# A hybrid decoder step: a shared third PSUM bank and partition prices in the order model, output norms on VectorE, sample-state updates in one array visit

## The chip, the core and the metric

The kernel runs on one core of a Trainium2 chip. The time is the device time of one execution in microseconds (us), as the median of several runs; smaller is better. The engines are TensorE (PE, with its weight loads as PEld), VectorE (DVE), ScalarE (ACT), GpSimd (POOL) and SyncE (SP), whose queue issues the DMA transfers here.

## The reference, cut to what matters

One layer of a decoder is computed in float32 for two sets of tokens at once: a prompt of 16 meta tokens and 512 new ones, and 8 short sequences of 8 tokens that start from given states (the samples). 592 token columns go through one input projection `z = x @ w_in` (2048 to 8320). The first 4224 columns feed 16 heads of 64 of a recurrent mixer (RWKV-7), the other 4096 feed 8 heads of 128 of a retention mixer. Each head's output is normalised, gated, and goes into the output projection `w_out` (2048 x 2048), and a layer norm closes the layer:

```python
def step(S, inp):                       # RWKV-7, per token
    r_t, w_t, k_t, v_t, kk_t, b_t = inp
    sa = jnp.einsum('bhvk,bhk->bhv', S, -kk_t)
    S = S * w_t[:, :, None, :] + sa[..., None] * b_t[:, :, None, :] + v_t[..., None] * k_t[:, :, None, :]
    return S, jnp.einsum('bhvk,bhk->bhv', S, r_t)
...
h = jnp.einsum('btc,cd->btd', jnp.concatenate([o_a, o_b], axis=-1).astype(x.dtype), w_out)
y = _layer_norm(ALPHA * x + h, ln_g, ln_b)
```

Results are the outputs y of the prompt and of the samples, and all new states.

## The kernel before, in words

**Work and tiles.** The transposed tokens x are held in two parts whose sum is x (XH rounded, XL the rest), and each weight chunk is split in the same way into wh (ScalarE) and wl (VectorE). A projection is thus three wide matmuls per 128 rows of K: XH with wh, XL with wh, XH with wl. The input projection runs over 65 units of 128 output columns: one shared unit, then for each of 8 pairs of RWKV heads p the units k, r, v, g of that pair and q, k, v, g of retention head p. A unit has two halves of tokens (272 and 320), which go to the banks pj[0] and pj[1] (printed bank_115 and bank_116 below), 48 wide matmuls each.

**Jobs.** All other work of a pair is done by generators that run beside the projection of later units. `gen_a` prepares the keys and decays and makes the products inside chunks of 64 tokens: for each of the groups of chunks 0 to 3, 4 to 7, 8 to 9 it takes two banks and alternates matmuls on the upper and the lower 64 rows of the array (heads 0 and 1). `gen_u` inverts the triangular parts, `gen_c` runs the recurrence over 9 chunks, with three products in each that hand over to ScalarE or VectorE (copies RHS, ZZ, the new state), `gen_s` updates the states of the samples, `gen_f` normalises the heads. `gen_b` is the retention head; it updates the samples' retention states with two matmuls of 96 rows and 512 columns.

In `gen_s`, ScalarE copies a first product into RSv, TensorE transposes RSv, and after two more products VectorE makes ZX[h], the update vectors of the 8 samples side by side (8 x 64 columns) for head h. One matmul per head of 64 x 512 outputs goes to one half of the bank n0: head 0 into partitions 0 to 63, head 1 into 64 to 127.

**What sets the order.** Nothing is scheduled on the chip: each engine runs its instructions as they were written, in order, and they wait for each other by semaphores. The class `Order` decides the written order while the program is built. It keeps a modelled clock per engine and a table of who reads and writes what, and an operation's earliest time is the end of what it depends on, plus a lag (`LAG`) and, when TensorE is the reader, SLACK = 200 ns more. After each wide matmul `pump` lets every live job, by priority, emit what is ready by that clock; a batch of small matmuls that uses the array in another shape (fewer rows or columns than 128) is let in only when all of the batch is ready. `ensure` forces a job on when the projection needs its result. Small products share two banks, m0 and m1 (bank_117 and bank_118), through `take` and `give`; r0 and r1 are the retention's, ob (bank_120) the recurrence's outputs, and sq (bank_119) serves only the transposition of x at the start and the output projection.

**Output projection.** 16 K-chunks times 4 column blocks of 512 times 5 token tiles (four of 128 tokens, and tile 4 with the 64 sample tokens, whose extra product uses 64 columns of the array). In the last column block the matmuls of the last ten K-chunks are done tile by tile: tile 0 goes along, then tiles 1, 2, 3 and 4 are caught up one after the other. When a bank is done, VectorE adds alpha times x (`gen_cell`), takes statistics, and after the last block `gen_stat` makes the mean and, with two POOL operations, the reciprocal root of the variance. `gen_norm` then normalises the four blocks of the tile: by the table SHARE tiles 0 to 2 and half of tile 3 take one ScalarE step, a VectorE product with the gain and a POOL addition of the bias, the rest of tile 3 and tile 4 two fused VectorE steps. Each block is stored by SP.

In the profile of before, VectorE, ScalarE and POOL instructions carry the helper's line 363, matmuls the lines 386 and 392; in the changed kernel these are 380, 403 and 409.

Of the kernel before, what the change touches and what calls it, by code (L numbers as in the profile page):

```python
# [12 lines left out]
ACTF = mybir.ActivationFunctionType  # L13
ALU = mybir.AluOpType
# [14 lines left out]
NPAIR = 8  # L29
RAW_BUFS = 3  # L30
HI_BUFS = 4
SLACK = 200.0
AHEAD = -300.0
RUN = 1200.0
DRAIN = 90.0
LAND = 2400.0
LAND_BIG = 2400.0
LD = 4
# [1 line left out]
NPRIO = 1  # L40
OPRIO = 1
FIRST = 200.0
SHARE = "ggggggggggggggdddddd"
LATE = 5
EARLY = 14
BACKLOG = {0: 4000.0, 1: 1000.0, 2: 500.0, 3: 300.0, 4: 100.0}

_CSPEC = [("ident", 128), ("ind", 2), ("mS", 64), ("mSs", 64), ("mQ", 64), ("mQs", 64),
# [62 lines left out]
class Op:  # L111


    __slots__ = ("eng", "ns", "reads", "writes", "emit", "size")

    def __init__(self, eng, ns, reads, writes, emit, size=None):
        self.eng, self.ns, self.emit, self.size = eng, ns, emit, size
        self.reads, self.writes = [_box(a) for a in reads], [_box(a) for a in writes]


def _box(ap):


    t = ap.tensor
    dims = ap.ap
    if ap.space == bass.MemoryType.DRAM:
        return (t.name, 0, 1, ap.offset, ap.offset + sum((n - 1) * abs(s) for s, n in dims) + 1)
    if ap.space == bass.MemoryType.PSUM:
        return (t.name, -1, 0, 0, 1)
    pitch = 1  # L130
    for d in t.shape[1:]:
        pitch *= d
    p0, c0 = divmod(ap.offset, pitch)
    return (t.name, p0, p0 + dims[0][1], c0, c0 + sum((n - 1) * abs(s) for s, n in dims[1:]) + 1)


def _is_ap(x):
# [19 lines left out]
class Order:  # L157
# [6 lines left out]
    def __init__(self):  # L164
        self.clock = {k: 0.0 for k in ("PE", "DVE", "ACT", "POOL", "SP", "AQ", "DMA")}
        self.mem = {}
        self.job = None
        self.live = []
        self.stage = {}
        self.first = 0.0  # L170
        self.shape = (128, 128)
        self.tiles = [[0.0, 0.0] for _ in range(16)]
        self.issued = (0.0, 0.0)

    def lag(self, src, dst, raw):
        if src == dst:
# [3 lines left out]
    def ready(self, op):  # L180
# [7 lines left out]
                        t = max(t, end + self.lag(eng, op.eng, w and not isw))  # L188
        return t

    def emit(self, op):
        ns = op.ns
        start = max(self.clock[op.eng], self.ready(op))
        end = start + ns
        if op.eng == "PE":
            end = self.array(op, self.ready(op))
        self.clock[op.eng] = end
        if op.eng in ("SP", "AQ"):
            end = max(end + 1300.0, self.clock["DMA"]) + op.size / 270.0
# [207 lines left out]
def kernel(ctx, tc, x_prompt, x_sample, state_rwkv, state_shift, state_ret, meta_tokens, w_in, w_out,  # L407
# [138 lines left out]
    bank = [psum.tile([128, 512], F32, name=f"bank{i}") for i in range(8)]  # L546
    pj = [bank[0], bank[1]]
    m0, m1, sq, ob, r0, r1 = bank[2:]
    free = [m0, m1]

    o_d = dram.tile([16, 128, 576], F32, name="o_d")
    lt_d = [dram.tile([4, 10, 32, 32], F32, name=f"lt_d{i}") for i in range(2)]
# [23 lines left out]

    def give(*b):
        od.call(lambda: free.extend(b))

    lock = [1]  # L580

# [282 lines left out]
    def gen_s(p):  # L864
# [30 lines left out]
            tt(OO_[rows, 512:576], n0[rows, rows], RSs[64:128, rows], ALU.add)  # L895
        for h in range(2):
            tt(ZX[h], ZZ[:, 9, h, :].unsqueeze(1).to_broadcast([128, 8, 64]), C["bm"].unsqueeze(2).to_broadcast([128, 8, 64]))
            mm(n0[64 * h:64 * h + 64, :], BT[:, 9, h, :], ZX[h].rearrange("p b v -> p (b v)"))
        tt(S0T, n0, S0T, ALU.add)
        give(n0)  # L900
        mark(f"S{p}", 3)
# [189 lines left out]
    korder = [i for p in range(NPAIR) for i in ((p, 8 + p) if p < NPAIR - 1 else (8 + p, p))]  # L1091
    KO = len(korder)
    tiles = range(5)
    cells = [(n, t) for n in range(4) for t in tiles]
    j_in = len(chunks)
    for i in range(EARLY):
        events.append(("out", len(chunks), 0, i, (0, 1)))
        chunks.append(("out", korder[i], 0))
    for n in range(4):
        for i in range(KO):  # L1100
            events.append(("out", len(chunks), n, i, (2, 3, 4) if n == 0 and i < EARLY else tiles))
# [51 lines left out]
    with tc.manual_schedule():  # L1153
# [130 lines left out]
        def gen_stat(t):  # L1284
            rows = trows(t)
            mv = MV[0:rows, t, :]
            V.bn_aggr(out=mv, in_=ST6[0:rows, t].rearrange("p a b -> p (a b)"))
            rs = RSTD[0:rows, t:t + 1]
            ts(rs, mv[:, 1:2], 1.0, 1e-5, e=G)
            tt(rs, rs, NEGH[0:rows, 0:1], ALU.pow, e=G)  # L1290
            nm = NM[0:rows, t:t + 1]
            if set(SHARE[4 * t:4 * t + 4]) != {"d"}:
                stt(nm, mv[:, 0:1], -1.0, rs)
            od.call(lambda: od.start(f"N{t}", gen_norm(t), NPRIO))
            yield

        def gen_norm(t):
            rows = trows(t)
            rs, nm, mu = RSTD[0:rows, t:t + 1], NM[0:rows, t:t + 1], MV[0:rows, t, 0:1]
            dst = y_prompt[0, 128 * t:128 * t + 128, :] if t < 4 else xsamp_y  # L1300
            for n, step in ((0, 0), (1, 0), (0, 1), (2, 0), (1, 1), (0, 2), (3, 0), (2, 1), (1, 2), (3, 1), (2, 2), (3, 2)):
                sl = slice(512 * n, 512 * n + 512)
                hw = hh[0:rows, t, sl]
                who = SHARE[4 * t + n]
                if who == "d":
                    if step == 0:
                        stt(hw, hw, mu, lng[0:rows, sl], ALU.subtract, ALU.mult)
                    elif step == 2:
                        stt(hw, hw, rs, lnb[0:rows, sl], ALU.mult, ALU.add)
                elif step == 0:  # L1310
                    act(hw, hw, ACTF.Identity, rs, nm)
                elif step == 1:
                    tt(hw, hw, lng[0:rows, sl])
                else:
                    tt(hw, hw, lnb[0:rows, sl], ALU.add, e=G if who == "g" else V)
                if step == 2:
                    S.dma_start(out=dst[:, sl], in_=hw)
            yield

        xsamp_y = y_sample.rearrange("b t d -> (b t) d")  # L1320
# [25 lines left out]
        for e, ev in enumerate(events):  # L1346
            stage["event"] = e
            j = ev[1]
            if ev[0] == "in":
                _, j, u, half, q, ui = ev  # L1350
                kind, p, s = u
                if half == 0 and q == 0:
                    if kind == "A" and s == "k":
                        od.start(f"A{p}", gen_a(p), 1)
                    if kind == "B" and s == "q":
                        od.start(f"B{p}", gen_b(p), 3)
                if q == 0 and ui:
# [15 lines left out]
                        od.pump()  # L1373
            else:
                _, j, n, ki, some = ev
                od.ensure("o", ki + 1)
                if ki == 0:
                    if n == 0 and 4 in some:
# [7 lines left out]
                if n == 3 and ki >= KO - HELD:  # L1386
                    late += work[1:]
                    work = work[:1]
                    if ki == KO - 1:
                        work += sorted(late, key=lambda w: w[0])  # L1390
                for iw, (t, k_, jb) in enumerate(work):
                    b = obank[5 * n + t]
# [9 lines left out]
                    for i, (b_, x_, w_) in enumerate(todo):  # L1402
                        end = i == len(todo) - 1
                        mm(b_, x_, w_, start=(k_ == 0 and i == 0), stop=(k_ == KO - 1 and end))
                        if k_ == KO - 1 and end:
                            stage["out"] = 5 * n + t + 1
# [44 lines left out]
```

## Time and profile before

| | us |
|---|---|
| median of 3 runs (lowest, highest) | 1382.36 (1382.06, 1383.02) |
| the profiled execution | 1382.55 |
| its span, first to last instruction | 1380.8 |
| TensorE busy | 1331.4 |
| VectorE busy | 884.0 |
| ScalarE busy | 644.7 |
| POOL busy | 72.5 |

The mean granted TensorE clock is 0.991 of full speed. All times below are us from the start of the span. A row of the timeline gives the start, the length, engine, line, operation, `out<-in` by tile names, the part of the array (rows*columns) for matmuls, partitions x elements, how many equal instructions in a row it stands for, and in brackets the idle time ahead of it with the instruction that ended it. A float32 matmul that is not split appears as two records, one for each pass. A row of the stretches has the start and end, the length, then the busy time of PE, PEld, DVE, ACT and POOL, the granted clock, the DMA share and GB/s.

### The profile page before, as it was taken

How to read it: one execution, taken by the hardware profiler on the slowest of the kernel's cores; microseconds unless marked ns; L12 is line 12 of the kernel's file. 1: busy time of each engine (PE TensorE's matmuls, PEld its weight loads, DVE VectorE, ACT ScalarE, POOL GpSimd, SP SyncE). 2: the span in 40 equal slices, each digit the busy share in tenths (PEclk: the TensorE clock that was granted, in tenths of full speed). 3: DMA queues.
4: the chain of work that ended last, by engine and by line, in shares of the span. 5: the costliest groups of instructions: out<-in, count | busy, mean ns of one | idle time of the engine just before them, and what ended most of it. 6: DMA issues, size and time to landing. Idle time of an engine off the chain costs nothing.

```text
span 1380.8 us, 26964 instructions
## 1 busy us (share of the span) xinstructions
PE 1331.4 (96%) x10392; PEld 1230.1 (89%) x10392; DVE 884.0 (64%) x2158; ACT 644.7 (47%) x1519; POOL 72.5 (5%) x131
## 2 busy tenths in 40 slices
PE   7999999999999999999999999999999999999993
PEld 6999899989998999899989998999899987777782
DVE  5774677566766676667666765676567658624347
ACT  4534564366336633663356435643564366512121
POOL 0000000000000000000000000100010001000024
PEclk9999999999999999999999999999999999999997
DMA  7343224322432243224322432243224347654313
GB/s 238 87 109 90 69 74 118 94 66 72 118 87 73 66 123 85 75 65 120 84 81 64 118 80 81 63 118 85 80 62 120 88 138 214 195 166 117 98 48 122
DMA packets 232342, 139.79 MB, mean 101 GB/s; under 512 B 58668, under 2 KB 212102, under 8 KB 231238
## 3 DMA queue, kind: packets, MB, share of 16 engines
q1 hardware_dynamic: 232214, 138.08, 35.3%
q8 instruction: 81, 1.33, 0.4%
q14 instruction: 47, 0.39, 0.1%
HBM read 119.30 MB, written 18.74 MB: 100 GB/s over the span
## 4 chain that ended last, share of the span: by engine, by line
PE 81%; DVE 9%; ACT 6%; issue 3%; DMA 0%; POOL 0%; DVEq 0%; SPq 0%; ACTq 0%; POOLq 0%
PE bank L386 77%; DVE RW L363 5%; PE bank L392 4%; DVE wl L363 1%; ACT RW L363 1%; ACT SF L363 1%; ACT XH L363 1%; DVE MOM L363 1%; ACT RT L363 1%; ACT RHS L363 1%; ACT wh L363 1%; DVE RT L363 1%; ACT RSv L363 1%; DVE SHT L363 1%; DVE XL L363 0%
## 5 line engine op out<-in xcount | busy, mean ns | idle before, releaser
L386 PE MATMUL bank<-XH,wl 128*128 128x320 f32 (+3 forms) x2080 | 634.0, 305 | 2.1 <-DVE wl L363 2.1
L386 PE MATMUL bank<-XL,wh 128*128 128x320 f32 (+3 forms) x2080 | 629.1, 302 | 0.0
L386 PE MATMUL bank<-XH,wh 128*128 128x320 f32 (+3 forms) x2080 | 627.5, 302 | 1.2 <-ACT wh L363 1.2
L386 PEld LDWEIGHTS bank<-XL,wh 128*128 128x128 f32 x2080 | 391.9, 188 | 7.9 <-issue 6.3
L386 PEld LDWEIGHTS bank<-XH,wl 128*128 128x128 f32 x2080 | 392.9, 189 | 6.0 <-DVE wl L363 3.6
L386 PEld LDWEIGHTS bank<-XH,wh 128*128 128x128 f32 x2080 | 392.8, 189 | 3.0 <-ACT wh L363 1.4
L363 DVE TENSOR_TENSOR wl<-raw,wh 128x512 fp32r<-128x512 f32 x292 | 201.4, 691 | 203.0 <-ACT wh L363 200.1
L363 ACT ACTIVATE wh<-raw 128x512 fp32r<-128x512 f32 x292 | 184.1, 631 | 205.3 <-PE bank L386 178.6
L363 DVE TENSOR_TENSOR RW<-RW 120x84 f32<-120x84 f32 (+27 forms) x558 | 149.9, 272 | 19.5 <-ACT RW L363 4.0
L386 PE MATMUL bank<-RW 32*32 32x32 f32 (+6 forms) x1904 | 146.8, 242 | 2.9 <-DVE RW L363 2.0
L386 PEld LDWEIGHTS bank<-RW 32*32 32x32 f32 (+4 forms) x1904 | 108.9, 145 | 28.0 <-DVE RW L363 9.0
L363 ACT ACTIVATE RW<-bank 128x512 f32<-128x512 f32 (+8 forms) x218 | 93.2, 438 | 47.2 <-PE bank L392 33.3
L363 ACT ACTIVATE RT<-bank 64x320 f32<-64x320 f32 (+9 forms) x122 | 47.7, 398 | 126.4 <-DVE RT L363 102.7
L363 ACT ACTIVATE SF<-RW,FT 64x64 f32<-64x64 f32 x144 | 49.7, 345 | 71.1 <-DVE RW L363 69.2
L386 PE MATMUL bank<-more,XH 128*128 128x512 f32 (+1 forms) x250 | 75.9, 395 | 0.0
L363 ACT ACTIVATE RW<-bank,OMM 128x272 f32<-128x272 f32 (+1 forms) x66 | 33.2, 502 | 68.9 <-PE bank L386 67.4
L386 PE MATMUL bank<-wh,XH 128*128 128x512 f32 x157 | 62.0, 396 | 0.0
L392 PE MATMUL bank<-CT,RW 128*128 128x128 f32 (+2 forms) x348 | 53.7, 282 | 8.2 <-DMA RW<-in_x_prompt_dram 7.5
L386 PE MATMUL bank<-wl,XH 128*128 128x512 f32 (+1 forms) x157 | 61.6, 394 | 0.0
L386 PEld LDWEIGHTS bank<-more,XH 128*128 128x128 f32 (+1 forms) x250 | 45.6, 183 | 12.4
L363 DVE TENSOR_TENSOR RW<-bank,N 64x128 f32<-64x128 f32 x80 | 22.5, 282 | 46.8 <-PE bank L386 45.7
L392 PEld LDWEIGHTS bank<-CT,RW 128*128 128x128 f32 (+2 forms) x348 | 41.2, 139 | 10.4 <-issue 7.5
(154 smaller groups left out, 1397.3 us busy)
## 6 DMA issues: line engine op xcount, KB each, us to landing
raw<-in_w_in_dram SPq DMA_DIRECT2D x259, 256.0 KB
raw<-in_w_out_dram SPq DMA_DIRECT2D x48, 256.0 KB
CT<-in_w_out_dram SPq DMA_DIRECT2D x30, 256.0 KB
RT<-in_state_ret_dram SPq DMA_DIRECT2D x8, 512.0 KB
out_dram<-RT SPq DMA_DIRECT2D x8, 512.0 KB
RW<-in_x_prompt_dram SPq DMA_DIRECT2D x16, 256.0 KB
out_dram<-RW SPq DMA_DIRECT2D x16, 256.0 KB
RW<-o_d SPq DMA_DIRECT2D x14, 288.0 KB
```

Source lines behind the costliest of these rows:

```text
L363: self.order.submit(Op(self.key, self.cost(name, n, kw, psum), reads, [out], lambda: f(*args, **kw)))
L386: lambda: self.eng.matmul(out, lhsT, rhs, start=start, stop=stop), (passes, move, load, shape, tiles)))
L392: lambda: self.eng.transpose(out, in_, ident), (1, move, _cols(in_) / 1.2, shape, tiles)))
```

## The change

1. The order model: SLACK goes from 200 to 100 ns; a new price SWITCH of 110 ns stands ahead of a VectorE or ScalarE operation whose first partitions (of its output and its first input) differ from those of the operation before it on that engine.
2. Bank sq joins m0 and m1 as a third shared bank; a job takes it back (`gen_keep`) when unit g of the last RWKV pair starts, and the output projection waits for that.
3. In `gen_s` the two 512-column matmuls become eight of 128 columns that alternate between the heads, after both ZX are made.
4. The last column block is done in the tile order 4, 0, 1, 2, 3. Tile 4 goes along with the K-chunks, tiles 0 to 3 are caught up after it.
5. The norms take neither ScalarE nor POOL: for each tile VectorE does four steps with the mean and the gain, then four with the reciprocal root and the bias. The stores become jobs of their own.

```diff
-SLACK = 200.0
+SLACK = 100.0
+SWITCH = 110.0
-SHARE = "ggggggggggggggdddddd"
+TURN = (4, 0, 1, 2, 3)
+KEEP = ("A", 7, "g")
...
+        self.rows = tuple(_row(a) for a in writes + reads[:1])
...
+    def switch(self, op):
+        return SWITCH * (op.eng in ("DVE", "ACT") and self.rows.get(op.eng) != op.rows)
...
     def emit(self, op):
         ns = op.ns
-        start = max(self.clock[op.eng], self.ready(op))
+        start = max(self.clock[op.eng] + self.switch(op), self.ready(op))
+        self.rows[op.eng] = op.rows
...
-    free = [m0, m1]
+    free = [m0, m1, sq]
...
+    def gen_keep(b):
+        while not any(x is b for x in free):
+            yield
+        free[:] = [x for x in free if x is not b]
+        yield
...
         for h in range(2):
             tt(ZX[h], ZZ[:, 9, h, :].unsqueeze(1).to_broadcast([128, 8, 64]), C["bm"].unsqueeze(2).to_broadcast([128, 8, 64]))
-            mm(n0[64 * h:64 * h + 64, :], BT[:, 9, h, :], ZX[h].rearrange("p b v -> p (b v)"))
+        for i in range(4):
+            for h in range(2):
+                mm(n0[64 * h:64 * h + 64, 128 * i:128 * i + 128], BT[:, 9, h, :], ZX[h][:, 2 * i:2 * i + 2].rearrange("p b v -> p (b v)"))
...
-    cells = [(n, t) for n in range(4) for t in tiles]
+    cells = [(n, t) for n in range(4) for t in (TURN if n == 3 else tiles)]
...
-            for n, step in ((0, 0), (1, 0), (0, 1), (2, 0), (1, 1), (0, 2), (3, 0), (2, 1), (1, 2), (3, 1), (2, 2), (3, 2)):
-                ...
+            for n in range(4):
+                stt(hh[0:rows, t, cut(n)], hh[0:rows, t, cut(n)], mu, lng[0:rows, cut(n)], ALU.subtract, ALU.mult)
+            for n in range(4):
+                stt(hh[0:rows, t, cut(n)], hh[0:rows, t, cut(n)], rs, lnb[0:rows, cut(n)], ALU.mult, ALU.add)
+                od.call(lambda n=n: od.start(f"W{t}{n}", gen_put(dst[:, cut(n)], hh[0:rows, t, cut(n)]), 0))
...
+                    if (kind, p, s) == KEEP:
+                        od.start("keep", gen_keep(sq), 0)
...
-                        work += sorted(late, key=lambda w: w[0])
+                        work += sorted(late, key=lambda w: TURN.index(w[0]))
```

What this moves on the engines is shown at three places. The first is VectorE at the end of the program (RW holds the outputs, SHT the statistics). Before:

```order
L363 SCALAR_TENSOR_TENSOR RW<-RW,bank_121 64x512
L363 TENSOR_TENSOR RW<-bank_121,RW 64x512
L363 BN_STATS SHT<-RW 64x6
L363 BN_AGGR SHT<-SHT 64x2
L363 TENSOR_TENSOR RW<-RW 128x512 x2
L363 SCALAR_TENSOR_TENSOR RW<-RW,SHT 64x512 x4
L363 SCALAR_TENSOR_TENSOR RW<-RW,SHT 128x512
L363 SCALAR_TENSOR_TENSOR RW<-RW,SHT 64x512 x2
```

Now:

```order
L380 BN_AGGR SHT<-SHT 64x2
L380 SCALAR_TENSOR_TENSOR RW<-RW,SHT 64x512 x8
L380 SCALAR_TENSOR_TENSOR RW<-RW,bank_119 128x512
L380 BN_STATS SHT<-RW 128x6
L380 BN_AGGR SHT<-SHT 128x2
L380 SCALAR_TENSOR_TENSOR RW<-RW,SHT 128x512 x8
L380 SCALAR_TENSOR_TENSOR RW<-RW,bank_115 128x512
```

The 64-row tile stands before the four full ones, and each tile's eight norm steps follow its statistics in one piece, where steps of two tiles stood mixed before.

The second place is TensorE at the samples' state update of a middle pair (the rows with 64x512 before, 64x128 now). Before:

```order
L386 MATMUL bank_115<-XH,wl_106 128x272
L386 MATMUL bank_117<-RW 64x512
L386 MATMUL bank_118<-RW 128x128
L386 MATMUL bank_115<-XH,wh_102 128x272
L386 MATMUL bank_117<-RW 64x512
L386 MATMUL bank_115<-XL,wh_102 128x272
```

Now:

```order
L403 MATMUL bank_116<-XH,wl_106 128x320
L403 MATMUL bank_119<-RW 64x128 x8
L403 MATMUL bank_118<-RHS,RW 66x128
L403 MATMUL bank_116<-XH,wh_102 128x320
L403 MATMUL bank_116<-XL,wh_102 128x320
```

The two updates with a wide matmul between them became one piece of eight.

The third place is TensorE at the first group of chunk products of `gen_a` in the pair after it, eight matmuls that alternate between two banks. Now (before, the eight stood in one piece in every pair):

```order
L403 MATMUL bank_117<-RW 128x128
L403 MATMUL bank_118<-RW 128x128
L403 MATMUL bank_117<-RW 128x128
L403 MATMUL bank_118<-RW 128x128
L403 MATMUL bank_117<-RW 128x128
L403 MATMUL bank_115<-XH,wh_105 128x272
L403 MATMUL bank_118<-RW 128x128
L403 MATMUL bank_117<-RW 128x128
L403 MATMUL bank_118<-RW 128x128
L403 MATMUL bank_115<-XL,wh_105 128x272
```

A wide matmul now stands after the fifth of the eight; this is so in six of the eight pairs. The second group keeps its eight in one piece.

More of the change, by code (lines that the diff above doesn't have):

```diff
@@ L111 @@
 class Op:
-    __slots__ = ("eng", "ns", "reads", "writes", "emit", "size")
+    __slots__ = ("eng", "ns", "reads", "writes", "emit", "size", "rows")
     def __init__(self, eng, ns, reads, writes, emit, size=None):
         self.eng, self.ns, self.emit, self.size = eng, ns, emit, size
+        self.rows = tuple(_row(a) for a in writes + reads[:1])
         self.reads, self.writes = [_box(a) for a in reads], [_box(a) for a in writes]
@@ L134, in _box, with _row @@
     return (t.name, p0, p0 + dims[0][1], c0, c0 + sum((n - 1) * abs(s) for s, n in dims[1:]) + 1)
+def _row(ap):
+    pitch = 1
+    for d in ap.tensor.shape[1:]:
+        pitch *= d
+    return ap.offset // pitch
 def _is_ap(x):
@@ L173, in __init__ @@
         self.issued = (0.0, 0.0)
+        self.rows = {}
     def lag(self, src, dst, raw):
@@ L1093 @@
     tiles = range(5)
-    cells = [(n, t) for n in range(4) for t in tiles]
+    cells = [(n, t) for n in range(4) for t in (TURN if n == 3 else tiles)]
+    index = {c: i for i, c in enumerate(cells)}
     j_in = len(chunks)
@@ L1100 @@
         for i in range(KO):
-            events.append(("out", len(chunks), n, i, (2, 3, 4) if n == 0 and i < EARLY else tiles))
+            events.append(("out", len(chunks), n, i, (2, 3, 4) if n == 0 and i < EARLY else TURN if n == 3 else tiles))
             chunks.append(("out", korder[i], n))
@@ L1290, in gen_stat, with gen_put @@
             tt(rs, rs, NEGH[0:rows, 0:1], ALU.pow, e=G)
-            nm = NM[0:rows, t:t + 1]
-            if set(SHARE[4 * t:4 * t + 4]) != {"d"}:
-                stt(nm, mv[:, 0:1], -1.0, rs)
             od.call(lambda: od.start(f"N{t}", gen_norm(t), NPRIO))
+            yield
+        def gen_put(dst, src):
+            S.dma_start(out=dst, in_=src)
             yield
@@ L1298, in gen_norm @@
             rows = trows(t)
-            rs, nm, mu = RSTD[0:rows, t:t + 1], NM[0:rows, t:t + 1], MV[0:rows, t, 0:1]
+            rs, mu = RSTD[0:rows, t:t + 1], MV[0:rows, t, 0:1]
             dst = y_prompt[0, 128 * t:128 * t + 128, :] if t < 4 else xsamp_y
-            for n, step in ((0, 0), (1, 0), (0, 1), (2, 0), (1, 1), (0, 2), (3, 0), (2, 1), (1, 2), (3, 1), (2, 2), (3, 2)):
[L1302 to L1317, printed above, removed]
+            cut = lambda n: slice(512 * n, 512 * n + 512)
+            for n in range(4):
[3 more added lines that the diff above has]
+                od.call(lambda n=n: od.start(f"W{t}{n}", gen_put(dst[:, cut(n)], hh[0:rows, t, cut(n)]), 0))
             yield
@@ L1375 @@
                 _, j, n, ki, some = ev
+                od.ensure("keep", 99)
                 od.ensure("o", ki + 1)
@@ L1389 @@
                     if ki == KO - 1:
-                        work += sorted(late, key=lambda w: w[0])
+                        work += sorted(late, key=lambda w: TURN.index(w[0]))
                 for iw, (t, k_, jb) in enumerate(work):
-                    b = obank[5 * n + t]
+                    b = obank[index[n, t]]
                     if k_ == 0 and b in pj:
@@ L1405 @@
                         if k_ == KO - 1 and end:
-                            stage["out"] = 5 * n + t + 1
+                            stage["out"] = index[n, t] + 1
                         if iw == len(work) - 1 and end:
```

## The prediction

> **What bounds the kernel now.** I read the page's busy shares and chain first, then the table of stretches, then TensorE's own waits, then the last 50 us row by row.
>
> ```profile
> PE 1331.4 (96%) x10392; PEld 1230.1 (89%) x10392; DVE 884.0 (64%) x2158; ACT 644.7 (47%) x1519; POOL 72.5 (5%) x131
> PE 81%; DVE 9%; ACT 6%; issue 3%; DMA 0%; POOL 0%; DVEq 0%; SPq 0%; ACTq 0%; POOLq 0%
> 400.00:440.00 40.00, 38.68 (x376) 36.36 (x375) 18.60 (x45) 22.01 (x65) 0.21 (x1) 1.00 0.25 64
> 1357.20:1380.80 23.60, 0.00 (x0) 0.00 (x0) 18.40 (x21) 1.52 (x2) 8.90 (x9) 0.56 0.33 114
> ...
> PE bank L392 <- DMA RW<-in_x_prompt_dram: 7.5, 1, 7.5
> PE bank L386 <- ACT wh L363: 5.5, 7, 1.2
> PE bank L386 <- ACT RHS L363: 3.2, 10, 1.1
> PE bank L392 <- ACT RSv L363: 2.8, 8, 0.4
> PE bank L386 <- DVE wl L363: 2.1, 7, 0.6
> PE bank L386 <- DVE RW L363: 2.0, 8, 0.7
> ```
>
> TensorE is busy for 96% of the span. In a stretch from the middle it idles 1.3 of 40 us, at a granted clock of 1.00. So until TensorE's last matmul time is saved in two ways only: shorter occupation of the array, or removal of some of the waits in the last five rows (15.6 us together; the 7.5 us ahead of them is the first load). After 1357.20 TensorE does nothing, and 23.6 us follow in which VectorE is busy for 18.4. That tail is bound by VectorE and whatever it waits for.
>
> **The tail: norms on VectorE alone, small tile first.** The rows of VectorE at the first two token tiles of the last column block, TensorE's last matmul, and then tile 4 (64 rows) with what follows:
>
> ```profile
> 1331.72 0.69 DVE L363 SCALAR_TENSOR_TENSOR RW<-RW,bank 128x512 f32<-128x512 f32 x1 [5.83 <-PE bank L386]
> 1332.44 0.69 DVE L363 BATCH_NORM_STATS2 SHT<-RW 128x6 f32<-128x512 f32 x1
> 1333.17 0.26 DVE L363 BATCH_NORM_AGGREGATE SHT<-SHT 128x2 f32<-128x24 f32 x1
> ...
> 1338.68 0.69 DVE L363 SCALAR_TENSOR_TENSOR RW<-RW,bank 128x512 f32<-128x512 f32 x1 [0.16 <-PE bank L386]
> ...
> 1356.81 0.39 PE L386 MATMUL bank<-wh,XH 128*128 128x512 f32 x1
> ...
> 1361.52 0.67 DVE L363 SCALAR_TENSOR_TENSOR RW<-RW,bank 64x512 f32<-64x512 f32 x1
> 1363.67 0.26 DVE L363 BATCH_NORM_AGGREGATE SHT<-SHT 64x2 f32<-64x24 f32 x1
> 1365.65 6.58 DVE L363 SCALAR_TENSOR_TENSOR RW<-RW,SHT 64x512 f32<-64x512 f32 x2
> 1372.16 5.37 DVE L363 SCALAR_TENSOR_TENSOR RW<-RW,SHT 64x512 f32<-64x512 f32 x8
> ...
> 1364.01 1.10 POOL L363 TENSOR_SCALAR SHT<-SHT 64x1 f32<-64x1 f32 x1 [4.66 <-DVE SHT L363]
> 1365.20 0.94 POOL L363 TENSOR_TENSOR SHT<-SHT,NEGH 64x1 f32<-64x1 f32 x1
> 1366.11 4.91 POOL L363 TENSOR_TENSOR RW<-RW 128x512 f32<-128x512 f32 x4
> ```
>
> Two things are to be seen. The tile that TensorE finished at 1357.20 reaches VectorE only at 1361.52. And the row at 1365.65 holds two instructions in 6.58 us where eight of the same kind take 5.37 a little later: it stands beside POOL's four additions, 4.91 us, which the change removes.
>
> Worked out for the new order: a full tile costs VectorE 1333.43 - 1331.72 = 1.71 us to read the bank and make the statistics, and eight norm steps 5.37: 7.08. Tile 4 costs 1363.93 - 1361.52 + 5.37 = 7.78. From tile 4's last matmul on VectorE has 7.78 + 4 x 7.08 = 36.1 us to do. TensorE then has the four deferred tiles before it, each 1338.68 - 1331.72 = 6.96: 27.8. So VectorE ends 8.3 us after TensorE. All ScalarE steps of the norms are gone; ScalarE was not the limit there (1.52 us busy), and its work now costs VectorE nothing extra, as two fused steps replace three.
>
> To this comes POOL: two tiny operations per tile still make the reciprocal root. The first took 1.10 us beside VectorE's work and delayed nothing visible; the second ended at 1366.14, 0.49 us after the VectorE step of 1365.65 began. I take that row, 0.5 x 5 tiles = 2.5 us. The bounds are 0 (the four steps that need only the mean, 2.7 us, cover them) and both in full, 5 x 2.04 = 10.2. Behind VectorE's end stand 1380.80 - 1377.53 = 3.3 us of stores and closing, to which I add 0.5 since the last stores are now 256 KB and not 128. New tail 8.3 + 2.5 + 3.8 = 14.6 against 23.6: **9.0 us less** (12.0 less without interference and with 3.3; 1.3 less at the bad end).
>
> [...]
>
> **The state update: one visit.** Between the wide projection matmuls TensorE visits a job's small matmuls; what a visit costs is the time from the start of the wide matmul ahead of it to the next wide start, less one wide step (0.13, from 496.65 to 496.78 below).
>
> ```profile
> 444.07 0.37 PE L386 MATMUL bank<-XH,wh 128*128 128x272 f32 x1
> 444.37 1.07 PE L386 MATMUL bank<-RW 128*64 128x512 f32 x2
> 445.37 0.40 PE L386 MATMUL bank<-XL,wh 128*128 128x272 f32 x1
> ...
> 488.66 0.30 PE L386 MATMUL bank<-XH,wh 128*128 128x320 f32 x1
> 488.89 1.16 PE L386 MATMUL bank<-RW 64*128 64x128 f32 x16
> 489.98 0.41 PE L386 MATMUL bank<-XL,wh 128*128 128x320 f32 x1
> ...
> 496.65 0.29 PE L386 MATMUL bank<-XH,wh 128*128 128x258 f32 x1
> 496.78 0.28 PE L386 MATMUL bank<-XL,wh 128*128 128x258 f32 x1
> 496.99 0.89 PE L386 MATMUL bank<-RW 64*128 64x128 f32 x8
> 497.81 0.38 PE L386 MATMUL bank<-XH,wl 128*128 128x258 f32 x1
> ```
>
> One 512-column update (two passes, half the array's columns) costs 445.37 - 444.07 - 0.13 = 1.17 us, and there are two of them in each of eight pairs: 2.34 a pair. The new visit has eight updates of 128 columns, in turn on the two column halves. The trace has no such visit; the nearest is the one at 488.89: eight matmuls of 128 columns in two passes, in turn on the two row halves: 489.98 - 488.66 - 0.13 = 1.19. If the column halves run side by side like the row halves, a pair saves 1.15: **9.2 us less** in all. The bounds are 0 (no overlap: as much streaming as before) and 14 (a visit of 0.6, by the column-half visit in the next fence, which streams 32 columns).
>
> ```profile
> 429.97 0.55 PEld L386 LDWEIGHTS bank<-RW 128*64 128x64 f32 x16 [0.19 <-issue]
> ...
> 429.97 0.66 PE L386 MATMUL bank<-RW 128*64 128x32 f32 x16
> ```
>
> [...]
>
> **The new order of the rest.** The halved slack, the priced partition changes and the third bank move nearly every small job. Three consequences can be priced.
>
> First a cost: the order shown above splits the visit of eight row-half matmuls into five and three, in six of the eight pairs. Four such matmuls cost 497.81 - 496.78 - 0.13 = 0.90, eight 1.19: 0.07 for each and 0.61 for going in and out. Six more visits cost **3.7 us more**.
>
> Second a gain: two waits of before get more cover.
>
> ```profile
> L386 PE MATMUL bank<-XH 96*128 96x512 f32 x16 | 7.6, 473 | 4.7 <-ACT wh L363 4.3 <-ACT SF L363 0.4
> ...
> 480.07 0.56 ACT L363 ACTIVATE RW<-bank,VEC 64x256 f32<-64x256 f32 x1
> 480.66 0.53 ACT L363 ACTIVATE RW<-bank,OMM 128x320 f32<-128x320 f32 x1
> 481.09 0.43 ACT L363 ACTIVATE RW<-bank 128x320 f32<-128x320 f32 x1
> ```
>
> The retention state update (96 rows) waits 4.7 us in all and the transpose of RSv 2.8. By the two orders, 15 wide matmuls lie between the product that RSv is copied from and its transpose in a middle pair before, and 30 now. The partition price is real: ScalarE's instruction at 480.66 follows one on other partitions and starts 0.03 us after its end, the one at 481.09 stays on its partitions and starts 0.10 before the end, so the change costs 0.13; the model now charges 0.11 where it charged nothing, and that is what those waits were short of. Of the 7.5 us I take **4 less**; the bounds are 0 and 7.5.
>
> Third a cost: handoffs to TensorE are placed 0.1 us closer to their data. The recurrence alone has 9 chunks x 3 handoffs x 8 pairs = 216. Most pass through an instruction whose partition change is now charged, which gives the tenth back. I take **2 more**, with 0 and 216 x 0.1 = 21.6 as bounds. The third bank is costed at nothing: in the middle TensorE never stood still for a bank, it took other jobs' matmuls and the wide ones; if that cover failed, a wait would show on it as in the rows above.
>
> **Sum.** The profiled execution took 1382.55 us, of which the span is 1380.8; it is 0.19 above the median of the three runs. 1382.55 - 9.0 - 9.2 + 3.7 - 4 + 2 = 1366.05, against the median 1366.
>
> **Rivals.**
> POOL keeps blocking the norm steps: the tail at its bad end, 1.3 instead of 9.0 saved: 1374. For it the 6.58 us row, against it that this row had four large POOL operations behind the small ones. Chance 0.08.
> The column halves do not overlap: 9.2 us are missing, 1375. [...] Chance 0.06.
> The waits go nearly altogether: of the 15.6 us all but the 1.2 and 0.6 of the start vanish and no new ones come: 1382.55 - 9.0 - 9.2 + 3.7 - 13.8 = 1354. For it that the model now charges what it left out; against it the halved slack. Chance 0.08.
> Late handoffs, the slower side: in the recurrence each handoff comes 0.1 us too early and TensorE stands still for it, with the wide matmuls queued behind in its order: 1382.55 - 9.0 - 9.2 + 3.7 + 21.6 = 1390. It takes the whole gain from 14.5 / 216 = 0.067 us a handoff on. For it the 3.2 us that TensorE already waits for RHS; against it that this was ten waits out of all the handoffs. Chance 0.05.
> No difference: gains in the array are given back as waits elsewhere and the tail falls short. 0.03.
>
> **How the numbers follow.** The forecast itself, 0.70, has its own range of 1361 to 1371 (about 3 us either way for the tail and about 4 for the waits). To leave out no more than two in ten the range goes to 1357 on one side, half way to the vanished waits and beyond, and to 1375 on the other, where two rivals end. Differences under 0.2%, 2.8 us, count as none. Faster: 0.70 + 0.08 + 0.06 + 0.08 = 0.92; same 0.03; slower 0.05.
>
> **What would show it.** Tail: TensorE's last matmul some 14 to 15 us before the end, VectorE without a step above 1.3 us there, four tiles' norms 7 to 7.6 us apart. State: one visit per pair of 16 column-half passes of 128 columns, its matmuls in couples some hundredth of a microsecond apart, about 1.2 us long. Split: 30 row-half visits, not 24. Waits: those for RSv and for the 96-row update below half, the sum for RHS not above 5 us. Wrong it would be if RHS and DVE waits grew beyond 10 us, or VectorE's end lay more than 12 us behind TensorE's.

## The result and the profile after

The changed kernel takes 1345.17 us (median of 4, 1345.04 to 1347.60) against 1382.69 (4, 1382.06 to 1383.52) for the kernel before on the same chip: a ratio of 0.9732, 95% interval 0.9716 to 0.9749. The gain is 37.5 us; the forecast was 16.7, and its range ended at 1357. The profiled execution has a span of 1343.3 us at a mean clock of 0.997.

The page's busy times of the kernel after:

```profile
PE 1309.4 (97%) x10488; PEld 1230.2 (92%) x10488; DVE 879.8 (65%) x2168; ACT 634.4 (47%) x1505; POOL 55.3 (4%) x117
```

Its stretches, the one from the middle that the prediction showed of before, and the tail:

```profile
400.00:440.00 40.00, 40.00 (x401) 38.04 (x400) 23.83 (x62) 24.20 (x73) 1.58 (x3) 1.00 0.28 77
1329.30:1343.30 14.00, 0.01 (x1) 0.00 (x0) 8.20 (x13) 0.00 (x0) 1.68 (x2) 0.69 0.57 207
```

Its TensorE's own waits (us in total, times, longest):

```profile
PE bank L409 <- DMA RW<-in_x_prompt_dram: 7.6, 1, 7.6
PE bank L403 <- DVE RW L380: 4.7, 8, 1.1
PE bank L403 <- ACT RHS L380: 2.8, 3, 1.3
...
PE bank L409 <- ACT RSv L380: 0.3, 1, 0.3
```

The tail is 14.0 us (23.6 before). That leaves 37.5 - 9.6 = 27.9 us ahead of it: TensorE's last matmul ends at 1329.3 instead of 1357.2. The two waits that the prediction priced have gone (RSv 2.8 to 0.3; the 96-row update 4.7 to 0.1, a row further down), but the idle time in such lists is far too small to hold 27.9 us. Over the whole list it fell by some 5.

A second measure finds it, the one that the prediction used for single visits: from the start of the wide matmul ahead of a visit to the next wide start, less one wide step (0.147 us for 320 columns). It holds the visit's waits too. Summed over all visits of the input projection it is 245.7 us before (472 visits) and 213.8 after (460): 31.9 less. Between wide matmuls without a visit 5.0 us more are saved. Against that, the part from the input projection's last wide matmul to TensorE's last matmul became 8.5 us longer (219.8 to 228.3), and the start 0.5: 31.9 + 5.0 - 8.5 - 0.5 = 27.9. In that part the rest of the last pair's jobs runs beside the output projection; more of them is left now (137 small matmuls, 119 before), and all three waits for RHS of the list above lie there, between 1101 and 1161. The prediction has no term for it.

The 31.9 us are not seen in the idle column because a record is longer than a step, as TensorE's rows of the kernel before show:

```profile
432.78 0.31 PE L386 MATMUL bank<-XL,wh 128*128 128x320 f32 x1
432.92 0.31 PE L386 MATMUL bank<-XH,wl 128*128 128x320 f32 x1
433.95 0.47 PE L386 MATMUL bank<-XH 96*128 96x512 f32 x1 [0.72 <-ACT wh L363]
```

Wide matmuls start 0.14 us apart, so the 96-row one could have started at 433.07. It started at 433.95, 0.88 us late; the row owns up to 0.72, since a record of 0.31 us covers the first 0.16. Waits shorter than that don't appear at all, and TensorE counts as busy in them. A wait inside a visit can stay unseen in the same way. Eight row-half matmuls, the kind of which the prediction priced one visit at 1.19 us, stand in the same pair of the kernel before a second time:

```profile
492.27 0.31 PE L386 MATMUL bank<-XL,wh 128*128 128x320 f32 x1
492.51 1.41 PE L386 MATMUL bank<-RW 64*128 64x128 f32 x16
493.85 0.42 PE L386 MATMUL bank<-XH,wl 128*128 128x320 f32 x1
```

This visit costs 493.85 - 492.27 - 0.147 = 1.43 us: its second matmul, on the other row half, begins 0.25 us after the first, at 492.76, when a VectorE step has ended at 492.71; in the visit at 488.89 the two start 0.01 us apart. No idle time is booked. In the kernel after, all ten undivided visits of this kind cost about 1.18.

VectorE's rows at the end of the kernel after:

```profile
1309.32 0.69 DVE L380 SCALAR_TENSOR_TENSOR RW<-RW,bank 128x512 f32<-128x512 f32 x1
1316.38 0.68 DVE L380 SCALAR_TENSOR_TENSOR RW<-RW,bank 128x512 f32<-128x512 f32 x1
...
1330.48 0.68 DVE L380 SCALAR_TENSOR_TENSOR RW<-RW,bank 128x512 f32<-128x512 f32 x1
...
1332.22 5.39 DVE L380 SCALAR_TENSOR_TENSOR RW<-RW,SHT 128x512 f32<-128x512 f32 x8
```

Tiles follow 7.06 us apart, and VectorE ends at 1337.61, 8.3 us behind TensorE. TensorE's rows at the state update of a middle pair:

```profile
436.85 0.30 PE L403 MATMUL bank<-XH,wl 128*128 128x320 f32 x1
437.08 1.09 PE L403 MATMUL bank<-RW 128*64 128x128 f32 x16
438.11 0.43 PE L403 MATMUL bank<-RHS,RW 128*66 128x128 f32 x2
438.30 0.40 PE L403 MATMUL bank<-XH,wh 128*128 128x320 f32 x1
```

The new state visit, with a recurrence product in the same visit, costs 438.30 - 436.85 - 0.15 = 1.30 us.

### The profile page after: what moved, and what is told of

Its sections match the earlier page's. It is cut to its first block, busy times and chain, and to the rows that moved or that the text cites. A ratio compares the mean times of both kernels' runs of the same rounds, so it can differ in the third digit from the quotient of the medians.

```text
span 1343.3 us, 27153 instructions
## 1 busy us (share of the span) xinstructions
PE 1309.4 (97%) x10488; PEld 1230.2 (92%) x10488; DVE 879.8 (65%) x2168; ACT 634.4 (47%) x1505; POOL 55.3 (4%) x117
## 4 chain that ended last, share of the span: by engine, by line
PE 92%; DVE 5%; issue 1%; ACT 1%; DMA 0%; DVEq 0%; SPq 0%; ACTq 0%
PE bank L403 88%; PE bank L409 4%; DVE RW L380 3%; DVE wl L380 1%; DVE XL L380 1%; DMA RW<-in_x_prompt_dram 0%; DVE SHT L380 0%; ACT XH L380 0%; DVE XH L380 0%; ACT RT L380 0%; DVE RT L380 0%; ACT RSv L380 0%; ACT wh L380 0%; ACT SF L380 0%; ACT RHS L380 0%
## 5 line engine op out<-in xcount | busy, mean ns | idle before, releaser
L403 PE MATMUL bank<-XH,wl 128*128 128x320 f32 (+3 forms) x2080 | 626.1, 301 | 0.6 <-DVE wl L380 0.6
L380 DVE TENSOR_TENSOR RW<-RW 120x84 f32<-120x84 f32 (+26 forms) x544 | 137.9, 256 | 18.5 <-DMA RW<-lt_d 4.1
L403 PE MATMUL bank<-RW 32*32 32x32 f32 (+6 forms) x2000 | 137.0, 239 | 4.8 <-DVE RW L380 4.7
L380 ACT ACTIVATE RW<-bank 64x256 f32<-64x256 f32 (+8 forms) x218 | 93.2, 438 | 52.8 <-PE bank L403 29.1
L380 ACT ACTIVATE RW<-bank,OMM 128x272 f32<-128x272 f32 (+1 forms) x66 | 33.3, 504 | 45.6 <-PE bank L403 42.9
L403 PE MATMUL bank<-wh,XL 128*128 128x512 f32 x126 | 50.4, 400 | 1.4 <-DVE XL L380 1.4
```

Source lines behind the costliest of these rows:

```text
L380: self.order.submit(Op(self.key, self.cost(name, n, kw, psum), reads, [out], lambda: f(*args, **kw)))
L403: lambda: self.eng.matmul(out, lhsT, rhs, start=start, stop=stop), (passes, move, load, shape, tiles)))
```

## The experiments

Each edit stands against the kernel that its first word names: `b_` is the kernel before, `a_` the changed one. Pair periods are from one pair's first wide matmul to the next pair's (139.2 us in the middle of before, 134.6 after).

### One part alone on the kernel before

Two theories were put up. MODEL: the order model's new numbers (price and shorter handoff) make the middle's gain. BANK: the third bank does, by letting jobs stand side by side.

b_model, price and handoff alone:

```
-SLACK = 200.0
+SLACK = 100.0
+SWITCH = 110.0
...
+        return SWITCH * (op.eng in ("DVE", "ACT") and self.rows.get(op.eng) != op.rows)
...
```

> The kernel before with the new order model alone (slack 100 ns, partition changes priced at 110 ns), two shared banks, old state update, old end. Of the 37.5 us that the whole change saved, 9.6 lie behind TensorE's last matmul and 27.9 before it. Theory MODEL: most of those 27.9 that are not the state update (about 19) are waits of TensorE that the priced partition changes cover, so this run saves 15 to 19 us: 1364 to 1368 us. Theory BANK: the third bank frees the jobs from waiting for each other, and the model alone saves 0 to 5: 1378 to 1383 us.

1395.4 us, ratio 1.0094 (1.0079 to 1.0109): slower. Neither theory had that.

b_bank3, the bank alone:

```
-    free = [m0, m1]
+    free = [m0, m1, sq]
...
```

> The kernel before with the third shared bank alone. Theory MODEL: nothing in TensorE's order waited for a bank, 1380 to 1385 us. Theory BANK: 12 to 19 us less, 1364 to 1371 us.

1386.8 us, ratio 1.0032 (1.0020 to 1.0044). BANK falls.

b_state, the state's one visit alone:

```
-            mm(n0[64 * h:64 * h + 64, :], BT[:, 9, h, :], ZX[h].rearrange("p b v -> p (b v)"))
+        for i in range(4):
+            for h in range(2):
+                mm(n0[64 * h:64 * h + 64, 128 * i:128 * i + 128], BT[:, 9, h, :], ZX[h][:, 2 * i:2 * i + 2].rearrange("p b v -> p (b v)"))
```

> The kernel before with the samples' state update as eight matmuls of 128 columns in one visit, nothing else. Both theories: the visit costs about 1.2 us where two of 1.17 stood, 8 to 10 us less, 1373 to 1375 us. If the column halves did not overlap: 1382 us.

1427.8 us, ratio 1.0331 (1.0314 to 1.0348): 45 us slower, from an edit that shortens the work.

b_tail, norms and tile order alone:

```
-cells = [(n, t) for n in range(4) for t in tiles]
+cells = [(n, t) for n in range(4) for t in (TURN if n == 3 else tiles)]
...
```

> The kernel before with the new end alone: last column block in the order 4, 0, 1, 2, 3 and all norms on VectorE. Both theories: TensorE ends when it did (1357 us into the span), the tail shrinks from 23.6 to 14 us, 1372.5 to 1374 us.

1372.0 us, ratio 0.9924 (0.9909 to 0.9939): 10.4 us, half a us more than expected.

**What made two of them slower.** Stretches of b_state, from a middle pair (start:end, length, busy PE, PEld, DVE, ACT, POOL, granted clock, DMA share, GB/s):

```profile
488.00:493.40 5.40, 5.40 (x38) 5.28 (x37) 5.31 (x12) 3.92 (x8) 0.20 (x1) 1.00 0.04 11
493.40:495.30 1.90, 0.15 (x2) 0.00 (x0) 1.86 (x5) 0.42 (x1) 0.00 (x0) 1.00 0.57 167
495.30:497.70 2.40, 1.16 (x16) 0.97 (x16) 2.37 (x4) 0.21 (x1) 0.97 (x3) 1.00 0.41 115
497.70:499.10 1.40, 0.00 (x0) 0.00 (x0) 1.34 (x5) 1.32 (x4) 0.00 (x0) 0.59 0.38 109
499.10:501.00 1.90, 0.79 (x2) 0.50 (x2) 1.84 (x5) 0.20 (x1) 0.00 (x0) 0.50 0.08 25
501.00:502.20 1.20, 1.15 (x6) 0.93 (x6) 1.13 (x4) 0.00 (x0) 0.00 (x0) 0.50 0.63 178
502.20:508.50 6.30, 6.30 (x32) 5.71 (x33) 3.17 (x7) 0.00 (x0) 0.29 (x2) 0.52 0.12 47
508.50:513.00 4.50, 4.50 (x42) 4.38 (x43) 1.74 (x6) 1.24 (x3) 0.00 (x0) 1.00 0.33 57
```

Its rows of TensorE and ScalarE around them:

```profile
485.51 0.29 PE L386 MATMUL bank<-XH,wl 128*128 128x272 f32 x1
485.63 0.31 PE L386 MATMUL bank<-XH,wh 128*128 128x320 f32 x1
...
497.78 0.49 ACT L363 ACTIVATE RW<-bank,OMM 128x272 f32<-128x272 f32 x1 [2.27 <-DVE RW L363]
498.17 0.39 ACT L363 ACTIVATE RW<-bank 128x272 f32<-128x272 f32 x1
...
502.20 0.58 PE L386 MATMUL bank<-XH,wh 128*128 128x258 f32 x1
```

The first half of the pair's value projection has its last matmul at 485.51, and the other half begins at 485.63. ScalarE evacuates the first half's bank only at 497.78, 12.2 us later, and waited for VectorE then. The gate projection, next in order, needs this bank. The bank is free at 498.56, but small matmuls of the late chain stand in TensorE's order ahead of the gate and wait for VectorE twice more (2.65 and 1.13 us), so that the gate starts at 502.20. Between 493.4 and 502.2 there is no wide matmul; TensorE is busy for 3.25 of 8.8 us with what small work there is, VectorE throughout. From about 498.0 (0.59 on average in the row that it falls in) to about 508.2 the granted clock is half: 32 matmuls in 6.3 us, where the next 4.5 us take 42.

The code says why the bank is late. The value and gate of pair p may be evacuated only when the output step F of pair p-1 is done, since it still reads their buffers:

```
yield from until((f"A{p-1}", 1 if s == "k" else 3) if s in "kr" else (f"F{p-1}", 99))
...
if q == 0 and ui:
    od.ensure("evac", 2 * ui - 1 + half)
```

F ends a chain: inverse, nine recurrence steps, sample states, head norms. Where the written order lets that chain end too late, the gate projection is **held**. Before, the value's bank was evacuated 0.2 us after its projection in every pair. In b_state five pairs are held for 8.7 to 8.8 us, in b_model three of the later ones, every second, for 9.9 to 10.1 and one early one for 6.7. The changed kernel's rows of ScalarE and TensorE at the same place:

```profile
481.91 0.39 ACT L380 ACTIVATE RW<-bank 128x272 f32<-128x272 f32 x1
...
483.42 0.28 PE L403 MATMUL bank<-XH,wh 128*128 128x258 f32 x1
```

The bank is 7.8 us late there too, but free at 482.30 and needed at 483.42: not held, with 1.1 us to spare. This is the theory LATE VALUES of the next runs, against PARTS ADD.

### One part taken out of the changed kernel

a_bank2 (without the third bank: the line of b_bank3 turned round):

> The changed kernel without the third shared bank and the wait that takes it back; all else as changed. LATE VALUES (new theory): a pair's value projection may be evacuated only when the pair before has finished its output step, and the gate projection behind it needs that bank. In the two runs that became slower the evacuation came 12.2 to 13.6 us after the projection's end instead of 0.2, no wide matmul ran for 8.7 to 10.1 us, and TensorE's granted clock fell to half behind it; a pair with it took 146.8 us, one without 132.8. In the changed kernel it comes 7.8 us late, just inside the cover of about 8 us. Without the third bank the steps between take turns in two banks, and the written order has a held gate projection in all seven later pairs: 7 x 8 to 14 us more, 1400 to 1440 us. PARTS ADD (rival): every part has its own worth whatever the others are; the bank alone made the kernel 4.4 us slower, so without it 1338 to 1348 us.

1398.7 us, ratio 1.0119 (1.0104 to 1.0134). This is 1.3 below the range of LATE VALUES and far above that of PARTS ADD. Seven pairs are held, for 5.0 to 11.9 us. The bank that is worth nothing alone is worth 53.5 us here.

a_slack200:

```
-SLACK = 100.0
+SLACK = 200.0
```

> The changed kernel with the handoff time to TensorE back at 200 ns (100 as changed). LATE VALUES: a chain whose every hop is placed 0.1 us later ends later; the order written has the gate projection held in all seven later pairs, for less than without the bank: 7 x 5 to 8 us more, 1380 to 1400 us, with the value evacuations 9 us or more behind their projections. PARTS ADD: the handoff time is worth a few us at most by itself: 1345 to 1362 us and no held projection.

1376.4 us, ratio 0.9963 (0.9945 to 0.9981): 31 us slower than the changed kernel, a little less than the range; seven pairs held for 5.4 to 6.1 us, the value evacuations 14.7 to 15.4 us late. Its runs scatter more than the others (1370.4 to 1382.0 in ten), and with them the granted clock: 0.991 in the shortest, 0.979 in the three longest. In the profiled one the clock fell in five of the seven holds.

a_switch0:

```
-SWITCH = 110.0
+SWITCH = 0.0
```

> The changed kernel with the price for a change of partitions at 0 (110 ns as changed). No gate projection is held in its written order, so LATE VALUES expects no loss from that: value evacuations less than 7 us behind their projections, and the time follows from what the price is worth by itself. If the price is what made TensorE's visits cheaper: the pair period goes back from 134.6 to 137 to 139 us, 1361 to 1378 us. If the visits became cheaper by the shorter handoff, the bank or the state's one visit: 134 to 136 us a pair, 1341 to 1355 us.

1372.9 us, ratio 0.9934 (0.9919 to 0.9949). Nothing is held, evacuations follow after 0.2 us, and still 27.7 us are lost. All visits together cost 243.4 us, as before (245.7). In three places its granted clock fell to 0.50 for 3.4 us without any hold, which makes some 5 of the 27.7 us (an estimate: half of 10.2). TensorE's rows for the recurrence product by form, of a_switch0 and of the changed kernel (count, busy us, mean ns, idle ahead):

```profile
L403 PE MATMUL bank<-RHS,RW 128*66 128x128 f32 x144 | 29.9, 289 | 6.5 <-ACT RHS L380 5.1
```

```profile
L403 PE MATMUL bank<-RHS,RW 128*66 128x128 f32 x144 | 28.4, 278 | 2.9 <-ACT RHS L380 2.8
...
L403 PE MATMUL bank<-XH 96*128 96x512 f32 x16 | 7.1, 443 | 0.1
```

So in this order the price is what makes the visits cheaper: without it the model thinks ScalarE's and VectorE's results ready sooner than they are, and TensorE meets its small matmuls too early. The last row is the 96-row update that waited 4.7 us before.

a_state2 (the edit of b_state turned round):

> The changed kernel with the state of the short sequences updated in two visits of 512 columns again; all else as changed. No gate projection is held in its written order. By the prediction's sum two visits of 1.17 us against one of 1.19: 8 x 1.15 = 9.2 us more, 1354 us (1350 to 1358) under both theories; over 1365 or under 1348 us would say that the worth of the one visit depends on the order around it.

1347.8 us, ratio 0.9753 (0.9737 to 0.9769): 2.6 us, not 9.2. In five pairs the two 512-column updates now share one visit of 2.02 us, where before they made two, of 1.60 (with another product in it) and 1.18. The rest of the order falls otherwise too: all visits cost 5.2 us more than in the changed kernel (219.0), and the part behind the input projection 2.1 less.

a_tail0 (norms and tile order of before):

> The changed kernel with the norms and the tile order of the kernel before. The tail is behind TensorE's last matmul and has nothing to do with the order of the rest: 1345.2 + 9.0 to 10.4 = 1354 to 1356 us, the end 23.6 us behind TensorE's instead of 14.0. Under 1350 or over 1360 us would say that the parts are not apart here either.

1356.8 us, ratio 0.9811 (0.9796 to 0.9825): 11.6 us, 0.8 above the range. TensorE ends where it does in the changed kernel (1329.2). The tail is apart from the rest.

| part | alone on before, us | taken out of the changed kernel, us |
|---|---|---|
| price and shorter handoff | +13.0 | price +27.7, handoff +31.2 |
| third bank | +4.4 | +53.5 |
| state in one visit | +45.4 | +2.6 |
| tail | -10.4 | +11.6 |

Only the tail has a worth of its own. The right column sums to 126.6, where the whole change brought 37.5.

### Taking the hold away

The value projection can come later in the pair at no cost in work; the chain of the pair before then ends in time.

a_slack200_v and b_state_v, and their control b_v, all with the same line:

```
-        units += [("A", p, s) for s in "krvg"] + [("B", p, s) for s in "qkvg"]
+        units += [("A", p, "k"), ("A", p, "r"), ("B", p, "q"), ("A", p, "v"), ("A", p, "g"), ("B", p, "k"), ("B", p, "v"), ("B", p, "g")]
```

> The changed kernel with the 200 ns handoff, as in a_slack200, and one line more: a pair's eight projections in the order key, receptance, query, value, gate, key of the second half, its value, its gate, so that the value projection and the gate behind it come one projection (some 16 us) later. It does the same work. LATE VALUES: the pair before has then finished when the value bank is full, the evacuation follows at once, no gate projection is held: all that a_slack200 lost against the changed kernel comes back, 1336 to 1350 us against its 1376. SHORT HANDOFF (rival): the shorter handoff is what makes TensorE's visits cheaper, and the held gates only stand beside it: 1362 to 1378 us.

1343.0 us, ratio 0.9712 (0.9698 to 0.9727). All 33.3 us come back; evacuations follow after 0.2 to 0.4 us. LATE VALUES holds, SHORT HANDOFF falls.

> The kernel before with the one-visit state update, as in b_state, and with the value projection behind the second half's query. LATE VALUES: no gate projection is held (b_state held one in five pairs), the wide matmuls don't stop and the clock stays up: 1375 to 1395 us against 1427.8. If the one visit itself were what costs, 1415 to 1435 us.

1393.1 us, ratio 1.0080 (1.0063 to 1.0097): 34.7 us come back, nothing is held.

> The control of the two runs with the value projection one later: the kernel before with that line alone. Nothing is held in the kernel before, so LATE VALUES expects no gain: 1378 to 1398 us, the rest being how well an order written without the price for a change of partitions happens to fall. Under 1370 us would say that the later value projection is a gain by itself, whatever is held.

1399.5 us, ratio 1.0124 (1.0109 to 1.0139), 1.5 above the range, with nothing held. The line by itself costs 16.8 us here, so the five holds of b_state were worth about 34.7 + 16.8 = 51.5 us, 10.3 each, if the two add. The stretches above give an estimate of how: 8.8 - 3.25 = 5.55 us of idling, and half of the 7.9 us that TensorE was busy at half clock (0.79 + 1.15 + 6.0), 4.0 more.

a_v, the changed kernel with value and gate behind the second half's query and key:

```
+        units += [("A", p, "k"), ("A", p, "r"), ("B", p, "q"), ("B", p, "k"), ("A", p, "v"), ("A", p, "g"), ("B", p, "v"), ("B", p, "g")]
```

> The changed kernel (100 ns handoff, price of 110 ns, third bank, one state visit) with the value projection moved behind the second half's query and key projections. LATE VALUES: the changed kernel's value evacuations come 7.8 us behind their projection, at the edge of their cover, and the order has to write steps in haste ahead of that edge; with the edge gone a little is to be had: 1336 to 1343 us. PARTS ADD: nothing is held in the changed kernel, so nothing comes back: 1343 to 1349 us.

1348.2 us, ratio 0.9748 (0.9733 to 0.9762): no gain, though the evacuations now follow after 0.2 us. Here the range of PARTS ADD is right and that of LATE VALUES wrong: the edge by itself cost nothing.

### The price where nothing is held

The line of b_model_v, b_v2 and a_late1 moves value and gate further:

```
+        units += [("A", p, "k"), ("A", p, "r"), ("B", p, "q"), ("B", p, "k"), ("B", p, "v"), ("A", p, "v"), ("A", p, "g"), ("B", p, "g")]
```

> The kernel before with the price (110 ns) and the 100 ns handoff, as in b_model, and with the value and gate projections moved behind the query, key and value projections of the second half. Two banks, two state visits, the tail as before. PRICE (theory): an order written with the steps' real times makes TensorE's visits cheaper whatever else is changed, as long as no gate projection is held: 22 to 32 us under its control b_v2, and 1340 to 1355 us against b_model's 1395.4. TOGETHER (rival): the price needs the third bank or the one-visit state to be worth anything: within 8 us of b_v2, 1368 to 1385 us.

> The control: the kernel before with the moved projections alone (no price, 200 ns handoff). Nothing was held in the kernel before, so both theories expect about its time or somewhat more, as in b_v (1399.5): 1370 to 1398 us.

1354.0 us (0.9793, 0.9777 to 0.9810) against 1369.1 for its control (0.9907, 0.9892 to 0.9921). The price and handoff alone, with two banks, old states and old tail, bring 15.1 us once nothing is held, and 41.4 against b_model, of which the line's own gain is 13.3. The gain over the control lies between the two theories' ranges; the time itself is inside that of PRICE, the control's 0.9 below its own. Visits cost 208.9 us against 233.1.

a_late1 (the line, SLACK 200, SWITCH 115 on the changed kernel) and a_late2 (order k r q v k v g g, 200 and 100):

> The changed kernel with the same moved projections, the 200 ns handoff and a price of 115 ns. PRICE: the price is near the time the traces show for a change of partitions, the long handoff costs nothing where no gate projection is held (a_slack200_v: 1343.0 us), and with two more projections of cover the steps between need no haste at all: 1328 to 1342 us. TOGETHER: 1343 to 1352 us, as a_slack200_v and a_v.

> The changed kernel with key, receptance, query, value, key and value of the second half, gate, gate: the gate projection is the one moved far, the value projection by one. 200 ns handoff, price 100 ns. PRICE: 1328 to 1343 us, as a_late1; TOGETHER: 1343 to 1352 us.

**1332.1 us** (0.9639, 0.9624 to 0.9653) and 1336.8 (0.9671, 0.9656 to 0.9685): both lie in the ranges of PRICE and beat the changed kernel, a_late1 by 13.1 us. Its page and TensorE's waits:

```profile
PE 1302.8 (98%) x10488; PEld 1228.7 (92%) x10488; DVE 883.1 (66%) x2168; ACT 632.6 (48%) x1505; POOL 58.8 (4%) x117
...
PE bank L409 <- DMA RW<-in_x_prompt_dram: 7.7, 1, 7.7
PE bank L403 <- DVE wl L380: 1.6, 3, 0.6
PE bank L403 <- DVE RW L380: 1.5, 6, 0.3
```

The wait for RHS (2.8 us in the changed kernel) is gone. Visits cost 205.3 us in 490 visits, less than the 213.8 in 460.

a_late0, a_late1 without the price:

```
-SWITCH = 115.0
+SWITCH = 0.0
```

> a_late1 (1332.1 us) with the price at 0 instead of 115 ns; third bank, one-visit state, new tail and the moved projections stay. BANK OR STATE: beside them the price is worth what a_switch0 showed, 24 to 32 us: 1356 to 1364 us. FALL OF THE ORDER: with nothing held the price is worth what it was on the kernel before, 12 to 18 us: 1344 to 1351 us.

1371.5 us, ratio 0.9923 (0.9906 to 0.9940): the price is worth 39.4 us here, more than either range; visits cost 232.8 instead of 205.3, and between wide matmuls 13.9 us more are lost as well. As in a_switch0, the clock fell three times for 3.4 us. That the price's worth grows beside bank and state agrees with BANK OR STATE, but three values (15.1, 27.7, 39.4) in three orders don't say how much of the growth is theirs. That stays open, as does why the later projections alone were worth 13.3 us in b_v2 and cost 16.8 in b_v.

## Why the prediction was wrong, point by point

- **Tail, -9.0: right.** 9.6 by the rows, 10.4 and 11.6 by the runs. Inside it two terms were off and nearly cancelled, which is luck: POOL's small operations delayed VectorE by nothing (2.5 taken; the eight VectorE steps beside them took 5.39 us, and VectorE ends 8.3 us behind TensorE, the sum without interference), and became longer themselves (0.75 and 0.93 us at the last tile, 0.19 and 0.55 at a full tile before). Behind VectorE's end stand 1343.3 - 1337.6 = 5.7 us, not 3.8. The rival of the blocked norms falls: the tiles lie 7.06 us apart.
- **State, -9.2: the mechanism right, the term too large.** The column halves run side by side: the sixteen matmul records at 437.08 start in couples 0.01 us apart, a couple about every 0.11 us, and their sixteen weight loads took 0.85 us beside 1.09 us of matmuls. A visit alone (the first pair's, nothing else in it) costs 1.12 us, 1.19 was taken, so the rival without overlap falls. But taken out of the changed kernel the edit is worth 2.6 us, in part since two old updates can share a visit (2.02 us); the term took it for granted that they never do.
- **Split, +3.7: right.** There are 30 row-half visits as forecast. In six pairs two visits of 0.96 and 0.83 us stand where one of 1.18 stood: 6 x 0.61 = 3.7. All such visits together still cost only 28.4 us instead of 28.0, because the others became 3.3 us cheaper, more than half of it by the loss of waits like the one at 492.76.
- **Waits, -4 ("The new order of the rest", second): the step that failed.** The prediction named the price real and what it would do, and bounded the gain by the 7.5 us that the idle rows of two waits show. Even the rival "the waits go nearly altogether" had only the 13.8 us of the list. The visits fell by 31.9. The state's one visit has a share in this (5.2 by a_state2). With the price taken out again the visits cost 243.4 - 213.8 = 29.6 us more and the kernel 27.7, in place of the 4 taken. The bound was wrong because the idle column leaves out 0.16 us of a wait behind a wide matmul, and shorter ones altogether. That this is all of the difference is not shown; the price changes the whole order.
- **Handoffs, +2.** No loss from the shorter handoff shows in the input projection: the waits for RHS in the list all lie behind it. It is worth 31.2 us in the changed kernel, by shortening the chain of every pair so that no gate projection is held; with the value projection later it is not needed (a_slack200_v, 1343.0).
- **Third bank, 0.** The reason given was that TensorE never stood still for a bank. It doesn't wait for this one either; the jobs that share the banks do, their chain ends later, and a different bank, the value's, then stops TensorE. In the changed kernel that is 53.5 us.
- **The slower side.** The rival of late handoffs did not come true, but two runs with parts of the change were slower by another mechanism: not TensorE a tenth early at each handoff but holds of 7 to 10 us in several pairs.
- **No term at all** stood for the last pair's jobs beside the output projection, which took 8.5 us of the gain back.

## What to carry to other kernels

Price waits from the distance between starts of the work that fills the engine, not from the idle column: where records overlap, the column hides the first part of a wait (0.16 of 0.88 us at 433.95). Where a planner writes the order, give it the price of each step that the trace shows, and look for the one dependence that runs from pair to pair. Here a chain that ended some 4 us later (12.2 us against 7.8) stopped the whole projection, and price and handoff made the kernel 13.0 us slower until that was out of the way, and 15.1 faster then. A part measured alone in such an order tells little on its worth beside the others; run it out of the changed kernel too.

## What the runs showed of the hardware

In b_state the granted clock fell to 0.50 at about 498.0, in a stretch of 8.8 us in which TensorE was busy for 3.25, and it stayed there until about 508.2, although TensorE was busy without a break from 502.2. At 0.50 the wide matmuls of 258 columns started 0.21 to 0.22 us apart (504.25 to 505.97); at 1.00, in the kernel before, two of them started 0.13 apart (496.65 and 496.78). TensorE was not idle all the time ahead of the fall: from 495.3 to 497.7 it was busy for 1.16 us. The clock was back 6.0 us after the first wide matmul. Behind the 21 holds of the four held runs (b_state, b_model, a_bank2, a_slack200) at which the clock fell that took 3.3 to 6.6.

The 10.2 us at 0.50 are one length of several. A fall in b_model lasted as long (494.3 to 504.5), the three in a_switch0 3.4 us each, and the only one in the kernel before while TensorE still had matmuls to do 3.41 (18.78 to 22.19), with TensorE busy throughout. What sets these lengths no run here shows.

Nor did every hold cost clock: of the seven holds in a_slack200, 5.4 to 6.1 us long, two went without a fall, and the runs don't show why. In b_state the halved clock added, by the estimate above, about three quarters to what the idling itself cost (4.0 beside 5.55 us).
